# Sixteen modulation tiles and three short dependent chains: TensorE's early vector tiles placed around the second product, the last block finished one token half at a time

## The chip, the cores and the metric

The kernel runs on one core of one Trainium2 chip. The metric is the device time of one execution in microseconds (us); less is better. A core has five engines that run side by side, each through its own instructions in a fixed order: TensorE (PE, matrix products), VectorE (DVE), ScalarE (ACT), GpSimd (POOL) and SyncE (SP), whose queue starts most of the transfers from memory. An engine that meets an instruction whose input is not there waits, and everything behind it on that engine waits too.

## The reference

A decoder trunk with two layers, for 256 tokens of width 2048, in f32. Layer 0 mixes tokens with a causal conformer convolution, layer 1 with Mamba-2; each mixer is followed by a squared-ReLU MLP of inner width 8192. Cut to what matters:

```python
# layer i:
shift1, scale1, gate1, shift2, scale2, gate2 = split(silu(c) @ w_mod[i] + b_mod[i], 6)
u = rmsnorm(x, norm_mix_g[i]) * (1 + scale1) + shift1
x = x + gate1 * mixer(u)          # i = 0: conformer_conv, i = 1: mamba2
u = rmsnorm(x, norm_mlp_g[i]) * (1 + scale2) + shift2
x = x + gate2 * ((relu(u @ w1[i]) ** 2) @ w2[i])
# after both layers: rmsnorm(x, final_norm_g)

def conformer_conv(u, ...):
    v = u @ w_pw1 + b_pw1         # 2048 -> 4096
    a, gt = split(v, 2)
    v = causal_dwconv(a * sigmoid(gt), w_dw, b_dw)    # 31 taps
    return silu(layernorm(v, ln_g, ln_b)) @ w_pw2 + b_pw2

def mamba2(u, ...):               # at its end, for 8 groups of 512 channels:
    y = (y_scan + d_skip * xs) * silu(z)
    y = y * rsqrt(mean(y * y over the group) + eps) * norm_g
    return y @ w_out
```

The shifts, scales and gates are products of one vector, silu(c), with `w_mod` of 2048 x 12288 for each layer: much weight traffic for very little arithmetic. All weights come from memory once, as f32; for the products each is split into a rounded part `wh` and a remainder `wl`.

## The kernel before

The five products (pw1 and pw2 of the conformer, w1 and w2 of each MLP, w_in and w_out of Mamba) stream their weights in tiles of 1 MB (128 x 2048 f32) through SP's queue. ScalarE makes `wh` of a half tile (line 361), VectorE makes `wl` (line 363), and TensorE multiplies both with the activations. Activations stand transposed, channels on the partitions and tokens along the row; `block` and `outer` issue those products (line 376). Only the second product of the last MLP is made by `block_t` the other way round (lines 430 to 432): its result has 128 tokens on the partitions, `q` = 0 and 1 being the two token halves, and 512 columns for each of the four blocks `b`. One weight tile of that block has two halves, so a block has eight halves, and each half gives six matmuls for each token half: two weight rows `k` by three (`wh` with the rounded activations, `wl` with them, `wh` with their remainder).

The vector products for shift, scale and gate are spread over the program. A job is a triple (layer, segment, tile), and `gemv` carries it out: it starts the 1 MB load (`stream`, line 347) into a buffer with the tag `wm` (two buffers) or `hid` (four), and then either VectorE multiplies and sums it (line 292), or, for the groups in `PE_GROUPS`, TensorE does it with four matmuls (line 283). Four such tiles make a group: ScalarE copies their row of sums (line 289), and `columns` turns it into columns with four transposes (line 304) and a sum. `PE_GROUPS` holds the four groups of `SH2`, the shift of layer 0's MLP: 16 tiles. `EARLY` is the list of the jobs of layer 0's beginning in the order in which they are taken; `pump(n)` takes the next n of it. `RATE_PW1` (how many before each weight tile of pw1), then `BETWEEN` (within the LayerNorm between the convolution and pw2) and `RATE_PW2` (before each weight tile of pw2) say how many are taken where.

A list scheduler (`tc`) sets each engine's order from the order in the program, priorities and a cost model; `issue_after(x)` puts what is in it behind x, and loads keep program order on SP's queue.

Three places in the program are chains of small steps, each of which waits for the one before on another engine, while TensorE has little or nothing else to do:

- The LayerNorm ahead of pw2: sums over channels by matmuls with ones (line 801), mean and root (lines 819 to 824), then Silu (line 842) and the rounding of the first activations (line 485), with which TensorE starts pw2 (line 376).
- The RMSNorm between pw2 and the MLP's first product: squares of the new residual (line 536), sums over channels by matmuls with ones (`ms<-ones,sq`, line 512), root and reciprocal, a diagonal matrix (line 499) that is multiplied with ones (line 503) to give the factor on all partitions, and the first activations (lines 488 and 489). The same chain stands after the first MLP and after Mamba.
- The end: `into_rows` adds the last block to the residual (lines 1045 and 1049), squares it (line 1050) and multiplies it by the final norm's weight (line 1051); then the factor for all 256 tokens is made (lines 1349 to 1351), both token halves are multiplied by it (lines 1356 and 1358), and four transfers of 512 KB write the output (line 1359).

In Mamba, w_in is made in 20 blocks. After each half weight tile's products `step` takes one step of a list of generators, `self.todo`: `scores`, `scan` and, for each group, `gated`. `gated` multiplies y by silu(z) (lines 1297 and 1299), squares it (line 1306 in the DVE rows) and adds the squares up in halves (lines 1309 and 1310), lets two steps pass (`yield from lag(2)`), and then has TensorE sum over channels (line 512) within the stream of w_in's products.

Of the kernel before, what the change touches and what calls it, by code (L numbers as in the profile page):

```python
# [15 lines left out]
P = 128  # L16
# [28 lines left out]


RATE_PW1 = [1, 1, 1, 1, 1, 2, 1, 1, 1, 2, 1, 1, 1, 1, 0, 0]
BETWEEN = 5
RATE_PW2 = [1] * 12 + [2, 1, 2, 1]
RATE_OPEN = [1] * 9 + [0] * 3  # L50
RATE_MLP = spread(80, 116) + [0] * 50
RATE_OUT = spread(24, 32)
# [12 lines left out]

EARLY = [(0, s, 4 * g + i) for s, g in ((G1, 0), (G1, 1), (G1, 2), (SC2, 0), (SH2, 0), (SH2, 1)) for i in range(4)]
_te = [(0, SH2, 5 + i) for i in range(11)]
_ve = [(0, G1, 12 + i) for i in range(4)] + [(0, SC2, 4 + i) for i in range(12)]  # L70
_mix = _ve[:1]
for _i in range(5):
    _mix += [_te[2 * _i], _ve[1 + _i], _te[2 * _i + 1]]
EARLY = EARLY[:-3] + _mix + _te[10:] + _ve[6:]


PE_GROUPS = {(0, SH2, g) for g in range(4)}
# [96 lines left out]
def lag(n):  # L174

    for _ in range(n):
        yield


class Trunk:  # L180
# [226 lines left out]
                    if j % 2:  # L407
                        self.step()

    def block_t(self, src, rhs, evac, pump=None):  # L410


        banks = [self.bank(self.mm, "mm") for _ in range(2)]
        mm = self.nc.tensor.matmul
        for g in range(4):
            w = self.load_w(src[g])
            if pump:
                with nullcontext() if g else self.tc.issue_after(self.evac):
                    self.pump(pump(g))
            with self.tc.high_priority(self.ahead):  # L420
                parts = self.split_w(w)
            for i, (wh, wl) in enumerate(parts):
                last = g == 3 and i == 1
                order = [(q, k) for q in range(2) for k in range(2)] if last else [
                    (q, k) for k in range(2) for q in range(2)]
                for q, k in order:
                    t = 2 * i + k
                    hi = rhs[g][:, t, q * Q:(q + 1) * Q]
                    lo = rhs[g][:, t, T + q * Q:T + (q + 1) * Q]
                    mm(banks[q], lhsT=hi, rhs=wh[:, k, :], start=g == 0 and t == 0, stop=False)  # L430
                    mm(banks[q], lhsT=hi, rhs=wl[:, k, :], start=False, stop=False)  # L431
                    mm(banks[q], lhsT=lo, rhs=wh[:, k, :], start=False, stop=g == 3 and t == 3)  # L432
                    if last and k:
                        evac(q, banks[q])
                self.step()
                self.step()

    def step(self):

# [111 lines left out]
    def conformer(self):  # L551
# [310 lines left out]
        def make(g):  # L862
            if g:
                normed(g)
            if g == 3:
# [3 lines left out]
                for b in range(4):  # L869
# [8 lines left out]
        self.outer([a["pw2"][b] for b in range(3)], make, lambda b, j, parts: into[b](j, parts), pump,  # L878
                   there=[(there[0], [half]), (there[1], ()), (there[2], ())])
        self.block(a["pw2"][3], v, into[3], pump=pump, single=True)  # L880
        return res["ss"]


# [66 lines left out]
    def mlp(self, layer, ss, pump=None, after=None, first=None):  # L950
        nc, a = self.nc, self.a
        with self.tc.high_priority(AHEAD_CHAIN):
            r = self.rstd_bcast(ss, D)
        u = []
        st = {"acc": [None] * 4, "ss": []}
        gate = lambda b: self.mod_tile(layer, G2, b)
        self.sq_row = self.t("mom", [P, 2, 4], bufs=1)

        def make(g):
            self.need(layer, SC2, SH2, kg=g)  # L960
            with self.tc.high_priority(0 if g else AHEAD_CHAIN):
                u.append(self.modulate(r, layer, SC2, SH2, g))
            return u[g]

        for c in range(4):
            hid = [None] * 4

            def act(b, j, parts):
                if hid[b] is None:
                    self.rings = ("wm",)  # L970
                    hid[b] = self.b("hid", [P, 4, 2 * T], F32R)
                s = self.total(parts)
                q = self.t("a", [P, T], bufs=3)
                if len(parts) == 1:
                    nc.scalar.activation(out=q, in_=s, func=AF.Relu)
                    s = q
                    nc.vector.tensor_mul(q, q, q)
                else:
                    nc.vector.scalar_tensor_tensor(out=q, in0=s, scalar=0.0, in1=s, op0=ALU.max, op1=ALU.mult)
                self.split_x(hid[b], j, q)  # L980

            if c == 0:
                self.outer([a["w1"][layer, b] for b in range(OPEN)], make, act, first or (lambda g: 0))
                if layer == 1:
                    self.todo.append(self.to_rows())
            for b in range(0 if c else OPEN, 4):
                self.block(a["w1"][layer, 4 * c + b], u, lambda j, parts, b=b: act(b, j, parts), pump=pump)
            if layer == 1:
                for b in range(4):
                    self.block_t(a["w2"][layer, c, b], hid, self.into_rows(b, c == 3))  # L990
                continue
            for b in range(4):
                if c == 3:
                    self.need(layer, G2)
                if b < 3:
                    ev = self.into_h(st, b, gate, after, acc=False) if c == 3 else None
                    self.block_t(a["w2"][layer, c, b], hid, self.into_turned(st, b, c, ev), pump=pump)
                    continue
                ev = self.into_h(st, b, gate, after) if c == 3 else self.into_acc(st, b, c == 0)
                self.block(a["w2"][layer, c, b], hid, ev, pump=pump, single=c == 3)  # L1000
        assert not self.todo
        return st["ss"]
# [35 lines left out]
    def into_rows(self, b, last):  # L1038

        nc = self.nc  # L1040

        def evac(q, bank):
            h = self.ht[q][:, b * 512:(b + 1) * 512]
            v = self.t("t2", [P, 512], bufs=3)
            nc.vector.tensor_mul(v, bank, self.gate_row[b])
            if not last:
                nc.gpsimd.tensor_tensor(out=h, in0=h, in1=v, op=ALU.add)
                return
            nc.vector.tensor_add(h, h, v)
            nc.scalar.activation(out=v, in_=h, func=AF.Square, accum_out=self.sq_row[:, q, b:b + 1])  # L1050
            nc.vector.tensor_mul(h, h, self.fg_row[b])
        return evac


    def mamba(self, ss):
# [246 lines left out]
    def gated(self, g, c):  # L1302

        nc = self.nc
        y, z = c["x"], c["z"]
        nc.vector.tensor_mul(y, y, z)
        sq = z
        nc.scalar.activation(out=sq, in_=y, func=AF.Square)
        nc.vector.tensor_add(sq[:, :2, :], sq[:, :2, :], sq[:, 2:, :])
        nc.vector.tensor_add(sq[:, 0, :], sq[:, 0, :], sq[:, 1, :])  # L1310
        yield from lag(2)
        r = self.rstd_cols([sq[:, 0, :]], 512)
        yield
        rs = self.spread(r)
        if g < 4:
            dst = y
        else:
            dst = self.late[g] = self.b("acc", [P, 4, T], bufs=5)
        for j in range(4):
            nc.vector.scalar_tensor_tensor(out=dst[:, j, :], in0=y[:, j, :], scalar=self.col("norm_g", 4 * g + j),  # L1320
                                           in1=rs, op0=ALU.mult, op1=ALU.mult)
            if g < 4:
                self.split_x(self.out_hl[g], j, dst[:, j, :])
            if j == 1:
                yield from lag(3)
# [11 lines left out]
    def run(self, out):  # L1337
        nc = self.nc
        ss = self.conformer()
        self.spare = 0  # L1340
        self.queue_mod(0, G2)
        self.queue_mod(1, SC1, SH1, *LATER)
        rate, first = iter(RATE_MLP), iter(RATE_OPEN)
        ss = self.mlp(0, ss, pump=lambda g: next(rate), first=lambda g: next(first))
        ss = self.mamba(ss)
        last = iter(RATE_LAST)
        self.mlp(1, ss, pump=lambda g: 1, first=lambda g: next(last))
        r = self.t("rcol", [P, 2])
        nc.vector.reduce_sum(out=r, in_=self.sq_row, axis=mybir.AxisListType.X)
        nc.scalar.activation(out=r, in_=r, func=AF.Sqrt, scale=1.0 / D, bias=self.eps)  # L1350
        nc.vector.reciprocal(r, r)
        for i in range(2):
            for q in range(2):
                v = self.ht[q][:, i * 1024:(i + 1) * 1024]
                if q:
                    nc.scalar.mul(out=v, in_=v, mul=r[:, q:q + 1])
                else:
                    nc.vector.tensor_scalar_mul(out=v, in0=v, scalar1=r[:, q:q + 1])
                nc.sync.dma_start(out=out[q, :, i * 1024:(i + 1) * 1024], in_=v)


def build(nc, tc, a, out):
    with ExitStack() as ctx:
# [17 lines left out]
```

## Time and profile before

| what | us |
| --- | --- |
| median of 3 runs | 2592.21 |
| the runs | 2587.94 to 2595.47 |
| profiled execution, its own time | 2593.28 |
| span of the profiled execution | 2591.2 |
| TensorE busy | 2540.7 |
| VectorE busy | 1910.9 |
| ScalarE busy | 1311.4 |

A row of the timeline reads: start and duration in us, engine, line, operation, output `<-` inputs, sizes, number of instructions, and in brackets how long the engine was idle before it and what released it. Matmuls are pipelined, so that the start of the next one, not the duration, gives the pace. A row of the table by stretches gives its length, then for each engine the busy time and the number of instructions, the clock that TensorE was granted (1.00 is full speed), the mean busy share of the 16 transfer engines, and what they moved in GB/s. The name before `<-` in a transfer is the buffer, the one behind it the array in memory. An instruction of SP in the timeline is the issue of a transfer; its landing is told apart.

### The profile page before, as it was taken

The page shows a single profiled execution, that of the slowest core. Times are in us where ns is not written, and L with a number is a line of the kernel's source. Part 1 is how long each engine was busy: PE and PEld are TensorE (multiplying, and loading weights), DVE is VectorE, ACT ScalarE, POOL GpSimd, SP SyncE. Part 2 cuts the span into 40 slices and gives each one's busy share as a digit, 9 for nine tenths or more (in the row PEclk, how much of TensorE's full clock was granted, in tenths as well). Part 3 has the DMA queues.
Part 4 walks back from the last instruction along what each step waited for, and adds up shares of the span by engine and source line. Part 5 has one row for each costly group of instructions (what it writes and reads, how often), then busy time and mean ns, then how long its engine had stood idle before and what let it go on. Part 6 is the DMA issues. An engine that isn't in the chain of part 4 may idle for free.

```text
span 2591.2 us, 36890 instructions
## 1 busy us (share of the span) xinstructions
PE 2540.7 (98%) x14671; PEld 2184.0 (84%) x14671; DVE 1910.9 (74%) x2460; ACT 1311.4 (51%) x2011; POOL 147.0 (6%) x212
## 2 busy tenths in 40 slices
PE   7999999999999999999999999999999999999998
PEld 5887698988888888888888888888998888888886
DVE  6579577877878878888777777898885555565565
ACT  2067453544434434447777667744454444443443
POOL 0011000000000000000000000000001101101000
PEclk8999999999999999999999999999999999999999
DMA  9988797788888878856555455688765555555553
GB/s 404 381 322 305 266 344 300 284 326 311 313 329 316 324 287 346 320 216 221 172 194 175 167 189 194 233 310 326 294 245 192 195 181 193 194 182 194 193 184 141
DMA packets 94895, 664.85 MB, mean 257 GB/s; under 512 B 10977, under 2 KB 10977, under 8 KB 16769
## 3 DMA queue, kind: packets, MB, share of 16 engines
q1 hardware_dynamic: 89138, 643.87, 67.4%
q0 software_dynamic: 5152, 16.97, 2.4%
q8 instruction: 115, 1.88, 0.3%
q10 hardware_dynamic: 432, 1.66, 0.2%
q14 instruction: 58, 0.48, 0.0%
HBM read 657.02 MB, written 2.20 MB: 254 GB/s over the span
## 4 chain that ended last, share of the span: by engine, by line
PE 93%; DVE 3%; DMA 2%; ACT 1%; issue 1%; POOL 0%; ACTq 0%; SPq 0%; DVEq 0%
PE mm L376 58%; PE mm L430 8%; PE mm L431 8%; PE mm L432 8%; PE mm L712 7%; DMA hid<-wmT 1%; PE mm L658 1%; DVE wl L363 1%; PE ms L712 1%; DMA wm<-wmT 1%; PE ms L1293 0%; PE ms L283 0%; DMA t<-eac_d 0%; DVE hid L292 0%; ACT wh L361 0%
## 5 line engine op out<-in xcount | busy, mean ns | idle before, releaser
L376 PE MATMUL mm<-u,wh 128*128 128x512 f32 (+1 forms) x4544 | 1376.5, 365 | 4.4 <-ACT u L485 2.3
L363 DVE TENSOR_TENSOR wl<-w,wh 128x1024 fp32r<-128x1024 f32 x768 | 942.2, 1229 | 506.1 <-ACT wh L361 500.3
L361 ACT CAST wh<-w 128x1024 fp32r<-128x1024 f32 x768 | 806.1, 1050 | 975.2 <-PE mm L376 589.5
L376 PE MATMUL mm<-u,wl 128*128 128x256 f32 x3840 | 1081.0, 282 | 0.1
L376 PEld LDWEIGHTS mm<-u,wh 128*128 128x128 f32 x4544 | 812.6, 190 | 156.1 <-issue 6.6
L376 PEld LDWEIGHTS mm<-u,wl 128*128 128x128 f32 x3840 | 730.5, 190 | 5.8 <-issue 2.5
L430 PE MATMUL mm<-wh,hid 128*128 128x512 f32 x896 | 351.0, 392 | 0.0
L432 PE MATMUL mm<-wh,hid 128*128 128x512 f32 x896 | 348.9, 389 | 0.0
L431 PE MATMUL mm<-wl,hid 128*128 128x512 f32 x896 | 348.8, 389 | 0.0
L292 DVE SCALAR_TENSOR_TENSOR wm<-wm,scb 128x2048 f32<-128x2048 f32 x132 | 301.7, 2286 | 11.4 <-DMA wm<-wmT 11.2
L712 PE MATMUL mm<-u,w 128*128 128x256 f32 x864 | 191.8, 383 | 18.7 <-ACT u L586 18.7
L712 PEld LDWEIGHTS mm<-u,w 128*128 128x128 f32 x864 | 164.7, 192 | 45.1 <-ACT u L586 19.9
L430 PEld LDWEIGHTS mm<-wh,hid 128*128 128x128 f32 x896 | 168.3, 188 | 35.8 <-issue 1.0
L431 PEld LDWEIGHTS mm<-wl,hid 128*128 128x128 f32 x896 | 168.3, 188 | 35.3 <-issue 0.7
L432 PEld LDWEIGHTS mm<-wh,hid 128*128 128x128 f32 x896 | 168.3, 188 | 35.1
L376 PE MATMUL mm<-hid,wh 128*128 128x512 f32 (+1 forms) x576 | 182.3, 373 | 0.0
L376 PE MATMUL mm<-hid,wl 128*128 128x256 f32 x512 | 144.1, 281 | 0.0
L292 DVE SCALAR_TENSOR_TENSOR hid<-hid,scb 128x2048 f32<-128x2048 f32 x44 | 100.5, 2287 | 41.7 <-DMA hid<-wmT 41.5
L376 PEld LDWEIGHTS mm<-hid,wh 128*128 128x128 f32 x576 | 104.1, 189 | 20.3 <-ACT u L485 0.2
L320 POOL TENSOR_TENSOR mod<-mod,par 128x4 f32<-128x4 f32 x46 | 37.1, 806 | 1128.8 <-DVE wm L292 915.2
L605 ACT ACTIVATE taps<-u,par 128x256 f32<-128x256 f32 x224 | 93.1, 500 | 9.2 <-DVE taps L614 6.7
L376 PEld LDWEIGHTS mm<-hid,wl 128*128 128x128 f32 x512 | 97.0, 190 | 0.4 <-issue 0.2
(251 smaller groups left out, 1606.0 us busy)
## 6 DMA issues: line engine op xcount, KB each, us to landing
w<-w SPq DMA_DIRECT2D x256, 1024.0 KB, 4.9
wm<-wmT SPq DMA_DIRECT2D x139, 1024.0 KB, 7.3
w<-win SPq DMA_DIRECT2D x80, 1024.0 KB, 4.9
hid<-wmT SPq DMA_DIRECT2D x53, 1024.0 KB, 10.5
w<-pw SPq DMA_DIRECT2D x46, 1024.0 KB, 6.9
w<-wout SPq DMA_DIRECT2D x32, 1024.0 KB, 6.9
acc<-ac_d POOLq DMA_DIRECT2D x16, 512.0 KB, 8.0
xpad<-u POOLq DMA_DIRECT2D x24, 131.5 KB, 8.1
```

The source lines that it names most:

```text
L292: self.sum = nc.vector.scalar_tensor_tensor(out=w, in0=w, scalar=1.0, in1=self.scb, op0=ALU.mult, op1=ALU.mult, accum_out=m[:, i:i + 1]).ins
L320: nc.gpsimd.tensor_tensor(out=m, in0=m, in1=b, op=ALU.add)
L361: nc.scalar.copy(out=wh, in_=w[:, s, :])
L363: nc.vector.tensor_tensor(out=wl, in0=w[:, s, :], in1=wh.bitcast(F32), op=ALU.subtract)
L376: self.pe = self.nc.tensor.matmul(out, lhsT=lhsT, rhs=rhs, skip_group_check=True, **kw).ins
L430: mm(banks[q], lhsT=hi, rhs=wh[:, k, :], start=g == 0 and t == 0, stop=False)
L431: mm(banks[q], lhsT=hi, rhs=wl[:, k, :], start=False, stop=False)
L432: mm(banks[q], lhsT=lo, rhs=wh[:, k, :], start=False, stop=g == 3 and t == 3)
L605: st["tap"] = nc.scalar.activation(out=p4[:, q, :], in_=vp[:, k + q:k + q + T], func=AF.Identity, scale=self.col("w_dw", ct * TAPS + k + q ...
L658: self.pe = nc.tensor.matmul(o[32 * c:32 * c + 32, :], lhsT=w[:, k, 32 * c:32 * c + 32], rhs=r[:, c, k:k + T], start=k == 0, stop=k == 7, ...
L712: self.pe = nc.tensor.matmul(o, lhsT=w[:, t, j * P:(j + 1) * P], rhs=u[g][:, t, :], start=g == 0 and t == 0 and j < 2, stop=g == 3 and t == 3,
```

## The change

Three edits:

- `EARLY` has a new order, and other numbers are taken at each place. In the LayerNorm seven `SH2` tiles are taken instead of five, in pw2 twelve jobs instead of 18 (five `SH2` tiles instead of eleven, and seven VectorE tiles as before), and a new `BEHIND` takes the last four `SH2` tiles behind pw2's last block, which is the RMSNorm ahead of the MLP.
- The last block of the last product takes `tail=5`: halves 5, 6 and 7 are kept back, and their 36 matmuls are issued with the 18 of token half 0 first. `into_rows` then ends each token half by itself (`rows_out`), with its own factor and its two output transfers. VectorE takes a half's first 1024 and last 512 columns, ScalarE the 512 between.
- `gated` lets three steps pass instead of two between its squares and their sum.

```diff
-BETWEEN = 5
-RATE_PW2 = [1] * 12 + [2, 1, 2, 1]
+BETWEEN, BEHIND = 7, 4
+RATE_PW2 = [1, 1, 1, 0] * 4
...
-EARLY = [(0, s, 4 * g + i) for s, g in ((G1, 0), (G1, 1), (G1, 2), (SC2, 0), (SH2, 0), (SH2, 1)) for i in range(4)]
-_te = [(0, SH2, 5 + i) for i in range(11)]
+_te = [(0, SH2, i) for i in range(16)]
 _ve = [(0, G1, 12 + i) for i in range(4)] + [(0, SC2, 4 + i) for i in range(12)]
-_mix = _ve[:1]
+EARLY = [(0, G1, i) for i in range(12)] + [(0, SC2, i) for i in range(4)] + _te[:7]
 for _i in range(5):
-    _mix += [_te[2 * _i], _ve[1 + _i], _te[2 * _i + 1]]
-EARLY = EARLY[:-3] + _mix + _te[10:] + _ve[6:]
+    EARLY += [_ve[_i], _te[7 + _i]]
+EARLY += _ve[5:7] + _te[12:] + _ve[7:]
...
-    def block_t(self, src, rhs, evac, pump=None):
+    def block_t(self, src, rhs, evac, pump=None, tail=8):
...
+            for i, hl in enumerate(parts, 2 * g):
+                if i >= tail:
+                    late.append((i, hl))
+                    continue
...
+        if late:
+            for q in range(2):
+                for i, hl in late:
+                    for k in range(2):
+                        sums(q, i, k, *hl)
...
         self.block(a["pw2"][3], v, into[3], pump=pump, single=True)
+        with self.tc.issue_after(self.pe):
+            self.pump(BEHIND)
...
-                    self.block_t(a["w2"][layer, c, b], hid, self.into_rows(b, c == 3))
+                    self.block_t(a["w2"][layer, c, b], hid, self.into_rows(b, c == 3), tail=5 if c == b == 3 else 8)
...
+    def rows_out(self, q, f):
+        nc = self.nc
+        r = self.t("rcol", [P, 2])[:, :1]
+        nc.vector.reduce_sum(out=r, in_=self.sq_row[:, q, :], axis=mybir.AxisListType.X)
+        nc.scalar.activation(out=r, in_=r, func=AF.Sqrt, scale=1.0 / D, bias=self.eps)
+        nc.vector.reciprocal(r, r)
+        row = self.ht[q]
+        nc.vector.tensor_scalar_mul(out=row[:, :1024], in0=row[:, :1024], scalar1=r)
+        nc.scalar.mul(out=row[:, 1024:1536], in_=row[:, 1024:1536], mul=r)
+        nc.vector.tensor_scalar_mul(out=row[:, 1536:], in0=f, scalar1=r)
+        for i in range(2):
+            cs = slice(i * 1024, (i + 1) * 1024)
+            nc.sync.dma_start(out=self.out[q, :, cs], in_=row[:, cs])
...
-        yield from lag(2)
+        yield from lag(3)
```

What this makes of the engines' orders is shown at three places. In these rows the numbers behind the names count buffers and differ between the two kernels, and the line numbers of the changed kernel are a few off: its line 282 is line 283 before, 375 is 376, 523 is 512, 514 is 503.

On SP's queue around the LayerNorm, before (`wm` and `hid` from `wmT` are vector tiles, `w` from `pw` is a weight tile of pw2; the first two rows are the fourth and fifth of the tiles that TensorE takes in the LayerNorm):

```order
L347 DMA wm_1928<-wmT 128x2048
L347 DMA hid_1936<-wmT 128x2048
L347 DMA w_267_1944<-pw 128x2048
L347 DMA wm_1952<-wmT 128x2048
L347 DMA hid_2008<-wmT 128x2048
```

And after:

```order
L346 DMA wm_1928<-wmT 128x2048
L346 DMA hid_1936<-wmT 128x2048
L346 DMA wm_1944<-wmT 128x2048
L346 DMA hid_1950<-wmT 128x2048
L346 DMA w_269_1956<-pw 128x2048
L346 DMA hid_1964<-wmT 128x2048
```

The loads of the sixth and seventh tile now stand ahead of pw2's weight tile. The sixth goes into a `wm` buffer, of which there are two; the buffer is that of the second tile.

On TensorE at the same place, before, from the third tile into pw2:

```order
L283 MATMUL ms_1911<-hid_1922,scol 32x512 x4
L283 MATMUL ms_1911<-wm_1928,scol 32x512 x4
L283 MATMUL ms_1939<-hid_1936,scol 32x512 x4
L376 MATMUL mm_1946<-u_1887,wh_1904 128x256
L376 MATMUL mm_1947<-u_1887,wh_1904 128x256
```

And after:

```order
L282 MATMUL ms_1911<-wm_1928,scol 32x512 x4
L282 MATMUL ms_1939<-hid_1936,scol 32x512 x4
L282 MATMUL ms_1939<-wm_1944,scol 32x512 x4
L375 MATMUL mm_1958<-u_1887,wh_1904 128x256
L375 MATMUL mm_1959<-u_1887,wh_1904 128x256
```

The sixth tile's four matmuls stand ahead of pw2's first, the seventh's thirteen rows behind it.

On TensorE in the RMSNorm ahead of the MLP, before (`ones` with `ssum` or `sq` are the sums of squares, `diag` is the factor's matrix, and the last row is the MLP's first product):

```order
L512 MATMUL ms_3123<-ones,ssum_2648 128x1 x2
L512 MATMUL ms_3123<-ones,sq_3103 128x1 x2
L376 MATMUL mm_2836<-u_2554,wh_3057 128x256 x2
L376 MATMUL mm_2836<-u_2554,wl_3058 128x256
L512 MATMUL ms_3123<-ones,sq_3112 128x1 x2
L512 MATMUL ms_3123<-ones,sq_3121 128x1 x2
L503 MATMUL ms_3137<-diag_3135,ones 128x256
L376 MATMUL mm_3140<-u_3146,wh_3171 128x256
```

And after:

```order
L282 MATMUL ms_3098<-hid_3095,scol 32x512
L523 MATMUL ms_3123<-ones,ssum_2648 128x1 x2
L523 MATMUL ms_3123<-ones,sq_3075 128x1 x2
L523 MATMUL ms_3123<-ones,sq_3084 128x1 x2
L282 MATMUL ms_3098<-hid_3095,scol 32x512 x3
L282 MATMUL ms_3098<-wm_3103,scol 32x512
L523 MATMUL ms_3123<-ones,sq_3093 128x1 x2
L282 MATMUL ms_3098<-wm_3103,scol 32x512 x3
L282 MATMUL ms_3098<-hid_3109,scol 32x512 x4
L282 MATMUL ms_3098<-hid_3115,scol 32x512 x4
L514 MATMUL ms_3137<-diag_3135,ones 128x256
L375 MATMUL mm_3140<-u_3146,wh_3171 128x256
```

Sixteen matmuls of the last four tiles stand between the sums, eleven of them behind the last sum and ahead of the product with `diag`.

On VectorE in `gated` of the first group, before (line 1240 is a mask added in another generator, 363 are splits of w_in's weights, 1306 to 1310 the squares and their halves):

```order
L1297 SCALAR_TENSOR_TENSOR wm_9823<-wm_9823,par,ms_10390 128x256 x2
L1240 TENSOR_TENSOR acc_10549<-acc_10549,mask 128x1024
L1299 TENSOR_TENSOR wm_9823<-wm_9823,t_1544_10245 128x4x128
L363 TENSOR_TENSOR wl_10461<-w_1578_10454,wh_10460 128x1024
L1306 TENSOR_TENSOR wm_9823<-wm_9823 128x1024
L363 TENSOR_TENSOR wl_10522<-w_1587_10519,wh_10521 128x1024
L1309 TENSOR_TENSOR wm_9823<-wm_9823 128x512
L1310 TENSOR_TENSOR wm_9823<-wm_9823 128x256
```

And after (1330 to 1343 are lines 1297 to 1310 of before):

```order
L1330 SCALAR_TENSOR_TENSOR wm_9823<-wm_9823,par,ms_10390 128x256 x2
L1332 TENSOR_TENSOR wm_9823<-wm_9823,t_1544_10245 128x4x128
L1339 TENSOR_TENSOR wm_9823<-wm_9823 128x1024
L362 TENSOR_TENSOR wl_10455<-w_1576_10448,wh_10454 128x1024
L1342 TENSOR_TENSOR wm_9823<-wm_9823 128x512
L1343 TENSOR_TENSOR wm_9823<-wm_9823 128x256
```

The mask and one split no longer stand between the gating and the squares. On TensorE the sum over channels of this group stands 13 matmuls nearer to the products of the generators ahead of it than before, since the scheduler has moved those as well.

More of the change, by code (lines that the diff above doesn't have):

```diff
@@ L408, in block, with sums @@
                         self.step()
-    def block_t(self, src, rhs, evac, pump=None):
+    def block_t(self, src, rhs, evac, pump=None, tail=8):
         banks = [self.bank(self.mm, "mm") for _ in range(2)]
         mm = self.nc.tensor.matmul
+        late = []
+        def sums(q, i, k, wh, wl):
+            g, t = i // 2, 2 * (i % 2) + k
+            hi = rhs[g][:, t, q * Q:(q + 1) * Q]
+            lo = rhs[g][:, t, T + q * Q:T + (q + 1) * Q]
+            mm(banks[q], lhsT=hi, rhs=wh[:, k, :], start=i == 0 and k == 0, stop=False)
+            mm(banks[q], lhsT=hi, rhs=wl[:, k, :], start=False, stop=False)
+            mm(banks[q], lhsT=lo, rhs=wh[:, k, :], start=False, stop=i == 7 and k == 1)
+            if i == 7 and k:
+                evac(q, banks[q])
         for g in range(4):
@@ L421, in block_t @@
                 parts = self.split_w(w)
[L422 to L434, printed above, removed]
+            for i, hl in enumerate(parts, 2 * g):
+                if i >= tail:
+                    late.append((i, hl))
+                    continue
+                for q, k in [(q, k) for q in range(2) for k in range(2)] if i == 7 else [
+                        (q, k) for k in range(2) for q in range(2)]:
+                    sums(q, i, k, *hl)
                 self.step()
                 self.step()
+        if late:
+            for q in range(2):
+                for i, hl in late:
+                    for k in range(2):
+                        sums(q, i, k, *hl)
     def step(self):
@@ L1050, in evac @@
             nc.scalar.activation(out=v, in_=h, func=AF.Square, accum_out=self.sq_row[:, q, b:b + 1])
-            nc.vector.tensor_mul(h, h, self.fg_row[b])
-        return evac
+            if b < 3:
+                nc.vector.tensor_mul(h, h, self.fg_row[b])
+                return
+            f = self.t("t2", [P, 512], bufs=3)
+            nc.vector.tensor_mul(f, h, self.fg_row[b])
+            self.rows_out(q, f)
+        return evac
+    def rows_out(self, q, f):
[11 more added lines that the diff above has]
+            nc.sync.dma_start(out=self.out[q, :, cs], in_=row[:, cs])
     def mamba(self, ss):
@@ L1346, in run @@
         last = iter(RATE_LAST)
+        self.out = out
         self.mlp(1, ss, pump=lambda g: 1, first=lambda g: next(last))
[L1348 to L1359, printed above, removed]
 def build(nc, tc, a, out):
```

## The prediction

> **What bounds the kernel now.** I read the page first: busy shares, the clock in forty slices, the chain that ended last.
>
> ```profile
> span 2591.2 us, 36890 instructions
> ...
> PE 2540.7 (98%) x14671; PEld 2184.0 (84%) x14671; DVE 1910.9 (74%) x2460; ACT 1311.4 (51%) x2011; POOL 147.0 (6%) x212
> ...
> PEclk8999999999999999999999999999999999999999
> ...
> PE 93%; DVE 3%; DMA 2%; ACT 1%; issue 1%; POOL 0%; ACTq 0%; SPq 0%; DVEq 0%
> ```
>
> TensorE is busy for 2540.7 of 2591.2 us. So an edit can win time in three ways only: fewer matmuls on that stream, less of the 50 us in which it stands still, or less time at a lowered clock, which the page's tenths are too coarse to show. I therefore went on to TensorE's timeline, and read every idle gap with its releaser, then stretches around the gaps for the clock.
>
> ```profile
> 304.37 1.06 PE L283 MATMUL ms<-hid,scol 128*32 128x512 f32 x8
> ...
> 307.83 1.04 PE L283 MATMUL ms<-hid,scol 128*32 128x512 f32 x8
> 311.15 0.85 PE L376 MATMUL mm<-u,wh 128*128 128x256 f32 x3 [2.28 <-ACT u L485]
> ...
> 420.84 0.61 PE L512 MATMUL ms<-ones,sq 128*128 128x1 f32 x4 [0.69 <-ACT sq L536]
> 422.69 1.19 PE L503 MATMUL ms<-diag,ones 128*128 128x256 f32 x2 [1.24 <-DVE diag L499]
> 424.99 1.22 PE L376 MATMUL mm<-u,wh 128*128 128x256 f32 x4 [1.11 <-ACT u L488]
> ...
> 1252.76 0.99 PE L512 MATMUL ms<-ones,wm 128*128 128x1 f32 x4 [2.54 <-DVE wm L1310]
> ...
> 1382.80 0.58 PE L512 MATMUL ms<-ones,wm 128*128 128x1 f32 x4 [0.70 <-DVE wm L1310]
> ```
>
> These are the gaps that the change touches: 2.28 us in the LayerNorm, 3.04 in the RMSNorm behind pw2, 2.54 and 0.70 at the channel sums of two gated groups. The clock around them:
>
> ```profile
> 306.46:309.87 3.41, 2.41 (x24) 0.52 (x16) 2.71 (x5) 1.95 (x3) 0.00 (x0) 1.00 0.73 231
> 309.87:313.28 3.41, 2.13 (x16) 1.97 (x17) 2.12 (x7) 3.41 (x9) 0.00 (x0) 1.00 0.94 351
> 419.10:422.51 3.41, 1.66 (x14) 1.49 (x13) 1.05 (x4) 2.14 (x4) 0.00 (x0) 1.00 0.21 87
> 422.52:429.32 6.80, 5.36 (x20) 4.38 (x21) 6.38 (x12) 2.11 (x5) 0.00 (x0) 0.50 0.66 253
> 1248.54:1251.95 3.41, 1.63 (x8) 0.90 (x6) 3.41 (x4) 2.92 (x7) 0.00 (x0) 1.00 0.61 196
> 1251.96:1258.76 6.80, 6.00 (x21) 5.35 (x22) 2.50 (x6) 5.57 (x8) 0.00 (x0) 0.50 0.70 249
> ```
>
> The columns are the stretch, its length, the busy time of PE, weight loads, DVE, ACT and POOL, the granted clock, and transfers. Two stretches of 6.8 us stand at half clock, and each follows a stretch of 3.41 us in which TensorE was busy for 1.66 or 1.63 us. Their starts, 422.51 and 1251.95, are 829.44 us apart, which is 243 times 3.413. I read this as a fixed grid of 3.41 us: a square of it that is half idle is paid with the next two at half speed. The LayerNorm's gap lies across a line of that grid (309.87 is 33 steps ahead of 422.51), which leaves 1.00 us idle in one square and 1.28 in the next, and the clock held at 1.00. So it counts how much of a gap falls into one square, and a longer gap in the same place is another matter.
>
> [...]
>
> **The tiles in pw2.** Eleven TensorE tiles stand within pw2's stream before and six after (the seventh of the LayerNorm and five). The price of one:
>
> ```profile
> 331.39 0.40 PE L376 MATMUL mm<-u,wh 128*128 128x256 f32 x2
> 331.63 0.28 PE L376 MATMUL mm<-u,wl 128*128 128x256 f32 x1
> 331.84 1.06 PE L283 MATMUL ms<-wm,scol 128*32 128x512 f32 x8
> 332.83 0.50 PE L376 MATMUL mm<-u,wh 128*128 128x256 f32 x2
> 333.17 0.28 PE L376 MATMUL mm<-u,wl 128*128 128x256 f32 x1
> ```
>
> Two matmuls of the stream take 0.24 us (331.39 to 331.63). From 331.63 to 333.17 are 1.54 us with three of them (0.36), so that a tile costs 1.18 us where the stream is full. Five fewer: −5.9 us. TensorE has no gap in pw2 before, so all of it shortens the path if nothing else becomes late. VectorE's tiles in pw2 stay seven, and the same megabytes come through SP's queue, in another order. I keep −5.3 to −6.5.
>
> **The sixth tile in the LayerNorm.** Five tiles run at 0.86 us each (304.37 to 307.83 is four) and end at about 308.7, when the second has long given back its `wm` buffer. The slot for the next `wm` load is there in the trace:
>
> ```profile
> 306.36 0.33 SPq L347 DMA_DIRECT2D wm<-wmT  x1
> 306.79 1.99 SPq L347 DMA_DIRECT2D hid<-wmT  x2
> ...
> L347 SPq DMA_DIRECT2D wm<-wmT x1: 328/328/328, 306.4 to 306.4; - x1
> ...
> DMA to landing us min/median/max: 6.4/6.4/6.4
> ...
> L347 SPq DMA_DIRECT2D wm<-wmT x1: 328/328/328, 1701.6 to 1701.6; - x1
> ...
> DMA to landing us min/median/max: 4.7/4.7/4.7
> ```
>
> Before, this load was for pw2. After, it carries the sixth tile, which stands ahead of pw2's first matmul. Issued at 306.36 with two more behind it, it landed 6.4 us later, at 312.76; a load of the same kind that had the queue to itself took 4.7 us, which would be 311.06. Then come 0.86 us of tile, and pw2 starts at 313.6 (or 311.9) instead of 311.15. I take +2.5 us, since the queue stands as in the first row; the lower end is +0.8. Behind the waiting tile on TensorE is all of pw2; the seventh tile lands about as far behind as one megabyte takes, 3 us at the 351 GB/s of the stretch from 309.87, while thirteen rows run. pw2's third weight tile goes behind both loads and is needed only with the third block's products; I cost it at nothing.
>
> With a landing at 312.76 the square from 309.87 to 313.28 is idle for 2.9 of 3.41 us, more than the 1.75 and 1.78 that were enough elsewhere. So the next two squares, 6.8 us of pw2, go at half speed: 3.4 us if TensorE is full all the time, 3.0 by the row of 1251.96 (6.00 busy). I take +3.0; with the early landing 1.2 us of that square are idle and it is 0. This term has the most doubt.
>
> **Four tiles in the RMSNorm behind pw2.** They go where TensorE waits anyway (0.69, 1.24 and 1.11 us), so their own time is mostly covered. But eleven of their matmuls stand between the last sum and the product with the diagonal: at 0.215 us each 2.4 us behind the sum at 420.84, which with its 0.43 gives 423.7 instead of 422.69, +1.0. What is late next is the first w1 product. In return the square up to 422.51 is full, and the half clock from 422.52 goes: the diagonal product takes 0.6 rather than 1.19, and the 4.3 us from 424.99 to 429.32 could take half. VectorE was busy for 6.38 of those 6.80 us, so I count 1.5 for both. −0.5 us, between −1.2 (all of the clock is won) and +0.5 (nothing but the wait).
>
> **Gated groups.** For the first group VectorE's and TensorE's orders move against each other.
>
> ```profile
> 1246.25 1.22 DVE L1240 TENSOR_TENSOR acc<-acc,mask 128x1024 f32<-128x1024 f32 x1
> ...
> 1249.12 1.22 DVE L1306 TENSOR_TENSOR wm<-wm 128x1024 f32<-128x1024 f32 x1
> ...
> 1252.19 0.42 DVE L1310 TENSOR_TENSOR wm<-wm 128x256 f32<-128x256 f32 x1
> ```
>
> A mask (1.1 us to the next start) and one split, also about 1.1, no longer stand ahead of the squares, so the last halving ends about 2.1 us earlier than at 1252.6. But TensorE reaches the sum 13 matmuls earlier, at 0.22 us some 2.8 us. So the wait of 2.54 becomes about 3.2, and the clock still drops: +0.7 us. Ends: −0.8 and +2.2, a split or two more or less ahead. For the other groups I count nothing.
>
> **The end.**
>
> ```profile
> 2578.15 0.39 PE L432 MATMUL mm<-wh,hid 128*128 128x512 f32 x1
> ...
> 2578.58 0.69 DVE L1045 TENSOR_TENSOR t<-mm,h 128x512 f32<-128x512 f32 x1
> ...
> 2580.03 0.63 ACT L1050 ACTIVATE t<-wm 128x512 f32<-128x512 f32 x1 [0.64 <-DVE wm L1049]
> ...
> 2582.11 1.42 DVE L1358 TENSOR_SCALAR wm<-wm,rcol 128x1024 f32<-128x1024 f32 x2
> ...
> L1359 SPq DMA_DIRECT2D out<-wm x4: 343/604/1176, 2582.9 to 2584.6; - x4
> ...
> DMA to landing us min/median/max: 2.7/4.9/5.6
> ```
>
> The last matmul stays at 2578.15, because the number of matmuls is the same. The four outputs are issued from 2582.9 to 2584.6, and the last lands at 2590.2. After, token half 0 ends some 4 us earlier (18 matmuls), and its two transfers are away before half 1's. Half 1 still goes through add, square, root and multiplication: its square starts at 2580.03 and is summed by 2580.8, reduction, root and reciprocal take about 0.7, so the multiplications start near 2581.5 instead of 2582.11. The first 1024 columns take 0.71 (half of 1.42); issues near 2582.3 and 2582.75. With two half megabytes instead of four in flight the last lands between 2586.2 (3.4 us behind its issue) and 2587.7 (4.9, the median of the four). I take 2586.9: −3.3 us, between −2.5 and −4.0.
>
> **The sum.** −5.9 + 2.5 + 3.0 − 0.5 + 0.7 − 3.3 = −3.5 us, against the profiled execution's 2593.28: 2589.8. That execution lay 1.07 us above the median of the three runs, 2592.21, so I predict 2588.7. If every term is at its good end, with the early landing and no drop, it is −6.5 + 0.8 + 0 − 1.2 − 0.8 − 4.0 = −11.7; at its bad end −5.3 + 2.5 + 3.4 + 0.5 + 2.2 − 2.5 = +0.8.
>
> **Rivals.**
> - The sixth tile is no wait to speak of: it lands near 311.1, the clock holds. For it: 4.7 us has been seen; against it: the row of 6.4 has the same neighbours in the queue. The two terms become 0.8 and 0, −8.2 in all: 2584.0. Chance 0.22.
> - The gated wait shrinks below what drops the clock. It needs VectorE 0.8 us earlier than I count, for instance by one more split moved behind the squares. Then the 2.54 is at most about 1.7 and the half clock goes: −0.8 − 3.0 instead of +0.7: 2584.2. Chance 0.12; together with the first, 2579.5, 0.04 more.
> - Slower: the sum of the squares comes too early in other groups as well. The row at 1382.80 shows a sum that waited 0.70 us. If TensorE gets to this one and to another some 2 us sooner, as to the first, each has a wait of about 2.7 and pays 3.0 of half clock: 5.0 and 5.7, together +10.7: 2599.4, and 2602 with the bad ends of two other terms. It decides from a wait of 1.75 us within one square on. Against it: VectorE's squares come earlier in all groups. Chance 0.07.
> - The end does not do what it says: half 1's transfers queue behind half 0's and land as late as before. Then −0.2 in all: 2592.0. Against it: half 0's would be issued near 2578.3, 4 us ahead. Chance 0.07.
>
> That leaves 0.48 for the forecast. A measurement of this kernel tells about 0.3%, 7.8 us, from no change, which puts the bounds at 2584.4 and 2600.0. Faster: two thirds of the first two rivals (0.22), their joint case (0.04) and a little of the forecast (0.02), 0.28. Slower: the third rival's upper half and the drift of three runs, 0.07. Same: 0.65. For 8 in 10 the range takes in both faster rivals and most of the third: 2579 to 2597.
>
> **What would show it.** In the trace after: TensorE's gap ahead of the sixth tile, 3 to 4 us from 308.7 on, and half clock from 313.3 to 320; pw2 from its first to its last product 5.9 us shorter but for that; no half clock behind pw2 and w1's products about half a microsecond late; the gated sum's gap near 3.2 us with half clock behind it; two pairs of output issues, four microseconds apart, and the last landing 8.7 us behind the last matmul's start instead of 12.1. I am wrong if the clock holds in pw2, or if pw2 has a gap of its own, with VectorE or a weight load as releaser.

## The result: 6 to 7 us slower

| | median, us | runs | range |
| --- | --- | --- | --- |
| before | 2592.29 | 22 | 2587.94 to 2598.44 |
| changed | 2599.17 | 22 | 2592.54 to 2602.35 |

The ratio is 1.0024, with an interval of 1.0017 to 1.0031: +6 us by the ratio (+4.4 to +8.0), +6.9 by the medians. I had predicted 2588.7. The lines of the changed kernel's page that answer to those shown of before:

```profile
span 2597.6 us, 36899 instructions
...
PE 2545.6 (98%) x14671; PEld 2181.9 (84%) x14671; DVE 1911.9 (74%) x2464; ACT 1310.6 (50%) x2013; POOL 145.7 (6%) x212
...
PEclk8999999999999999999999999999999999999999
```

The shares differ by one point at most; the clock in tenths and the count of matmuls are those of before. TensorE is busy 4.9 us longer, and the span is 6.4 us longer. To see where, I set the two traces against each other on TensorE: both have the same 5264 matmuls with a `wl` half, in nearly the same order, and the k-th of the one less the k-th of the other says how far the changed kernel is behind at that point. This table is worked out from the two traces, at places in the program:

| place (time before, us) | changed less before, us | step |
| --- | --- | --- |
| first products of pw2 (312) | +4.8 | +4.8 |
| pw2 at 353 | +5.1 | +0.4 |
| end of pw2 (414) | −0.5 | −5.6 |
| first MLP, 434 | +1.0 | +1.5 |
| first MLP, 514 | +3.1 | +2.1 |
| end of the first MLP (1142) | +4.0 | +0.9 |
| near the end of w_in (1643) | −1.6 | −5.6 |
| end of w_out (1849) | +11.1 | +12.7 |
| second MLP to the last product (2578) | +10.4 | −0.7 |
| end of the span (2591.2) | +6.4 | −4.0 |

One row is much larger than anything that I had in the sum: w_out, whose own code the change leaves as it is, loses 12.7 us. The other rows first, each with the lines that answer to those of the prediction.

In the LayerNorm (TensorE's timeline, the sixth tile's load, and stretches, all of the changed kernel):

```profile
308.08 1.04 PE L282 MATMUL ms<-hid,scol 128*32 128x512 f32 x8
313.92 1.94 PE L282 MATMUL ms<-wm,scol 128*32 128x512 f32 x8 [4.80 <-DMA wm<-wmT]
315.79 1.01 PE L375 MATMUL mm<-u,wh 128*128 128x256 f32 x3
...
L346 SPq DMA_DIRECT2D wm<-wmT x1: 328/328/328, 306.6 to 306.6; - x1
...
DMA to landing us min/median/max: 7.3/7.3/7.3
...
309.55:312.95 3.40, 0.00 (x0) 0.00 (x0) 2.14 (x6) 2.99 (x8) 0.00 (x0) 1.00 0.99 352
312.97:319.77 6.80, 5.85 (x28) 3.90 (x32) 4.17 (x5) 2.65 (x4) 0.00 (x0) 0.50 1.01 422
```

The sixth tile's load was issued at 306.61, as foreseen, landed 7.3 us later, and TensorE stood for 4.80 us; the square of 3.4 us ahead of 312.95 is wholly idle and the next 6.8 us run at half clock.

In the RMSNorm behind pw2:

```profile
421.59 0.61 PE L523 MATMUL ms<-ones,sq 128*128 128x1 f32 x4
422.12 1.06 PE L282 MATMUL ms<-wm,scol 128*32 128x512 f32 x3
422.95 1.08 PE L282 MATMUL ms<-wm,scol 128*32 128x512 f32 x3
423.00 3.60 PE L282 MATMUL ms<-hid,scol 128*32 128x512 f32 x15
426.52 0.70 PE L514 MATMUL ms<-diag,ones 128*128 128x256 f32 x2
428.34 0.91 PE L375 MATMUL mm<-u,wh 128*128 128x256 f32 x3 [1.11 <-ACT u L499]
```

The idle time is gone (but for 1.11 us), since the tiles fill it; but they stand ahead of the diagonal product, which starts 4.93 us behind the last sum's start instead of 1.85 before, and w1 begins at 428.34 instead of 424.99.

At the gated sums of groups 0 and 6:

```profile
1254.66 0.65 PE L523 MATMUL ms<-ones,wm 128*128 128x1 f32 x4 [3.29 <-DVE wm L1343]
...
1661.45 0.58 PE L523 MATMUL ms<-ones,wm 128*128 128x1 f32 x4 [1.13 <-DVE wm L1343]
...
1255.05:1258.46 3.41, 3.41 (x12) 2.93 (x12) 1.25 (x4) 1.28 (x3) 0.00 (x0) 0.50 0.66 271
1258.46:1261.87 3.41, 3.41 (x23) 3.08 (x22) 2.83 (x6) 1.32 (x3) 0.00 (x0) 1.00 0.32 46
```

Group 0 waits 3.29 us, about the 3.2 of the prediction. But the half clock behind it lasts one square of 3.41 us, not two as before, and so this place wins: from 1240 to 1259 the changed kernel goes from 3.8 us behind to 2.6. And the end:

```profile
2584.90 0.69 DVE L1058 TENSOR_TENSOR t<-mm,h 128x512 f32<-128x512 f32 x1 [1.77 <-PE mm L423]
...
2588.98 0.69 DVE L1058 TENSOR_TENSOR t<-mm,h 128x512 f32<-128x512 f32 x1
...
L1085 SPq DMA_DIRECT2D out<-wm x4: 332/356/383, 2588.6 to 2593.1; - x4
...
DMA to landing us min/median/max: 2.6/3.1/3.5
```

Token half 0's last steps start 4.08 us ahead of half 1's, the landings take 3.5 us at most instead of 5.6, and the span ends 9.1 us behind the last matmul's start (2588.55) instead of 13.1.

### The profile page after: what moved, and what is told of

The parts are those of the page before. It is cut to its first block, busy times and chain, and to the rows that moved or that the text cites. A ratio compares the mean times of both kernels' runs of the same rounds, so it can differ in the third digit from the quotient of the medians.

```text
span 2597.6 us, 36899 instructions
## 1 busy us (share of the span) xinstructions
PE 2545.6 (98%) x14671; PEld 2181.9 (84%) x14671; DVE 1911.9 (74%) x2464; ACT 1310.6 (50%) x2013; POOL 145.7 (6%) x212
## 4 chain that ended last, share of the span: by engine, by line
PE 91%; DVE 4%; DMA 3%; ACT 1%; issue 1%; POOL 0%; SPq 0%; DVEq 0%; ACTq 0%
PE mm L375 55%; PE mm L421 8%; PE mm L423 8%; PE mm L422 8%; PE mm L723 7%; DVE wl L362 1%; DMA hid<-wmT 1%; PE mm L669 1%; PE ms L723 1%; DVE hid L291 1%; PE ms L282 1%; DMA w<-wout 1%; DMA wm<-wmT 1%; PE ms L1326 0%; ACT wh L360 0%
```

## What w_out shows

w_out over 100 us, before and then changed (the columns are length, PE, weight loads, DVE, ACT, POOL, clock, share of the transfer engines, GB/s):

```profile
1660.00:1760.00 100.00, 100.00 (x599) 87.17 (x597) 93.19 (x122) 57.66 (x87) 2.93 (x5) 1.00 0.82 310
```

```profile
1660.00:1760.00 100.00, 94.66 (x551) 78.85 (x550) 88.50 (x124) 54.55 (x86) 2.75 (x4) 1.00 0.70 274
```

Before, TensorE never stops in these 100 us, and VectorE is busy for 93% of them: it splits w_out's weights, adds up results and takes vector jobs of layer 1, of which all of w_out has 24 at 2.29 us. In the changed kernel both are busy for less, and TensorE issues 551 matmuls instead of 599. From 1643 to 1849 the 12.7 us divide so, by the two traces: TensorE is idle for 5.7 us instead of 0.0; the groups' own matmuls there are 87 instead of 67, and take 2.4 us more, which w_in is spared; and w_out's products follow each other more slowly, 4.6 us in all. What stands differently there are the last two groups. The halving of group 6's squares on VectorE, before:

```profile
1640.26 0.42 DVE L1310 TENSOR_TENSOR wm<-wm 128x256 f32<-128x256 f32 x1
```

and changed:

```profile
1660.88 0.42 DVE L1343 TENSOR_TENSOR wm<-wm 128x256 f32<-128x256 f32 x1
```

It is 20.6 us later, while TensorE's stream is 1.6 us ahead there. Counting `yield`s in the code explains a part of it. Every `step` takes the next piece of the first generator in the list, whichever group it belongs to. A block takes 16 steps (two for each half weight tile, not one), so w_in's 20 blocks have 40 steps for each of the 8 groups, and a step lasts 25.5 / 16 = 1.6 us. A group's generators take 17 (`scores`) + 18 (`scan`) + 6 (`gated`) = 41 before (group 0 takes 44), and 42 with one more in `gated`. Once group 0 has begun, the list never runs empty, so the extra steps add up: group 6's squares stand six steps later than before (9.6 us) and its sum seven, group 7's seven and eight. Counted so, group 6 ends at step 312 of w_in's 320 instead of 305, and group 7 runs 34 steps into w_out instead of 26. The diff says "one step more"; the program makes it eight at the end. On VectorE the delay does not grow evenly: the last halvings of groups 0 to 7 start 1.9, 12.8, 4.7, 5.0, 9.7, 0.5, 20.6 and 18.2 us later than before. The scheduler's order and the waits come on top of the steps; how much each gives was not tried.

Two waits follow. The first is on SP's queue between 1600 and 1760 (total, times, longest): in the changed kernel the vector tile that stands ahead of w_out's third weight tile waits 13.5 us for a `wm` buffer that group 6 still holds, where it did not wait before (the 8.9 us of before are at group 7). Before and changed:

```profile
SPq L347 <- DVE acc L1320: 8.9, 1, 8.9
```

```profile
SPq L346 <- DVE acc L1353: 17.4, 2, 13.5
```

The second is on VectorE, which multiplies a scan's result with factors that come by a transfer (line 1284, now 1317), and stands still until they land; between 1628 and 1760, before and then changed:

```profile
DVE t L1284 <- DMA t<-eac_d: 2.9, 1, 2.9
```

```profile
DVE t L1317 <- DMA t<-eac_d: 10.9, 2, 6.2
```

VectorE stands still for 8 us more here; in the 100 us above it had 6.8 us to spare.

## The experiments

Two theories stood at first: that the extra step in `gated` makes w_out late (step theory), and that the moved early tiles do, through the vector jobs behind them (tile theory). Ratios are against runs of the kernel before in the same batch.

**The extra step taken back, and alone.**

```diff
 # x1: the changed kernel
-        yield from lag(3)
+        yield from lag(2)
 # x2: the kernel before
-        yield from lag(2)
+        yield from lag(3)
```

> The changed kernel with the gated groups' wait put back to two steps. Step theory: a group's generators take 41 steps before and 42 in the changed kernel, while w_in offers 40 for each group, so every group ends a step (1.6 us) later than the one before it, the last two run into w_out, and w_out loses about 11 us while w_in gains about 5. Then undoing it gives about 7 us: 2592 us, 0.0 to +0.05% against the kernel before, with the RMSNorm behind pw2 still 3.6 us slower and the end 4 us faster. Tile theory: the loss in w_out comes from the other places of the early tiles, through later vector jobs; then this stays near 2599.

> The kernel before with three steps instead of two in gated, nothing else. Step theory: +7 us, 2599, and w_out's products start as late as in the changed kernel (about 12 us lost there, 5 won in w_in). Tile theory: within 1 us of before.

Measured: x1 2589.38 us, ratio 0.9989 (0.9980 to 0.9998); x2 2602.27 us, ratio 1.0037 (1.0024 to 1.0049). One number in the code costs 9 to 10 us, whichever way it is tried, somewhat more than the 7 that I read from the two profiles. In x2's trace w_in ends 5.3 us ahead of before and w_out 9.5 behind; within w_out it has 3.4 us at half clock, from 1721.8 (its granted clock is 0.98 from 1660 to 1760), which the changed kernel's trace has not (1.00 in the row above). The tile theory has fallen.

**The end alone, the early tiles alone.** x3 is the kernel before with `tail=5` and `rows_out`; x4 is the kernel before with the new `EARLY`, `BETWEEN`, `RATE_PW2` and `BEHIND`.

> The kernel before with only the end changed (the last block one token half at a time, with its own output transfers). By the profile of the changed kernel, whose last landing came 9.3 us behind the last matmul's start instead of 13.1: -4 us, 2588. If what the end won there was only that the transfers met less traffic at that moment: 0 to -2.

> The kernel before with only the early tiles moved. By sums over the changed kernel's trace: LayerNorm +5.1, pw2 -5.6, RMSNorm and the first products behind it +3.6, mlp +1.0: +4 us, 2596. Tile theory: it also has w_out's loss, +11 to +15.

Measured: x3 2588.24 us, 0.9982 (0.9974 to 0.9991): −4.7 us (−6.7 to −2.3), as the profile's −4.0. x4 2592.63 us, 1.0004 (0.9994 to 1.0014): +1 us, less than the +4 that I read from one trace, and no difference that these runs can tell. The three parts add up: −4.7 + 1.0 + 9.6 = +5.9, against the +6 measured for all three.

**Is it the number of steps, or the pause in each `gated`?**

```diff
 # x5: the kernel before, in gated
-        yield from lag(2)
+        yield from lag(2 if g else 10)
 # x6: the kernel before, in gated and at the end of scan
-        yield from lag(2)
+        yield from lag(3)
...
-        yield from lag(2)
+        yield from lag(1)
```

> The kernel before, with ten steps instead of two between squares and sum in group 0 alone, and two in all the others. Step theory (what counts is how many steps all groups together have taken by the end): groups 6 and 7 come as late as in the changed kernel, w_out loses about 11 us, and w_in wins about as much as with three steps everywhere: +8 to +11, 2600 to 2603. If it is the place of the later groups' own sums that costs: those are as before, group 0's wait of 2.54 us and its half clock go, and the time falls by 3 to 5: 2588.

> The kernel before with three steps in gated and one step instead of two at the end of scan, just ahead of it, so that a group takes 41 steps as before. Step theory: the loss is gone; the time is that of before within 2 us, since sum and squares stand as before and only the gating is taken up a step earlier. If a longer pause within gated itself costs (the buffer that it holds for one step more): +8 to +10, as with three steps alone.

Measured: x6 2592.48 us, 1.0000 (0.9992 to 1.0009). The pause in `gated` is three steps as in x2, the sum of steps is 41, and the loss is gone: it is the sum that counts. x5 2594.77 us, 1.0005 (0.9996 to 1.0014), so both expectations missed. Its trace shows why. It wins 5.5 us at group 0 (from 1240 to 1280), where neither the wait of 2.54 us nor the half clock is left, and then w_out loses as it does with three steps everywhere: by 1639 it is 5.6 us ahead of before, by 1800 5.7 behind. The step theory had the loss right and group 0's gain too small.

**SP's queue, or VectorE's time?** Within w_out two causes were left: weights that stand in SP's queue behind a vector tile whose buffer is not free, or VectorE, that has no room. x7 keeps vector tiles out of the first quarter of w_out; x9 moves eight of them to the first MLP.

```diff
 # x7: the changed kernel
-RATE_OUT = spread(24, 32)
+RATE_OUT = [0] * 8 + spread(24, 24)
 # x9: the changed kernel
-RATE_MLP = spread(80, 116) + [0] * 50
-RATE_OUT = spread(24, 32)
+RATE_MLP = spread(88, 116) + [0] * 50
+RATE_OUT = spread(16, 32)
```

> The changed kernel, but with no vector job ahead of the first eight weight tiles of w_out, and one ahead of each of the other 24. SP theory: w_out starves since its weight loads stand in SP's queue behind a vector tile whose buffer group 6 still holds; then most of the loss goes, 2591 to 2594. Rival: VectorE and ScalarE have the last two groups' steps to do while they split w_out's weights, and the queue only follows; then 2597 to 2601.

> The changed kernel with 8 of the 24 vector jobs of w_out done in the first MLP instead (88 there, 16 in w_out). VectorE theory: w_out loses because VectorE, busy for 147 of 160 us there before, has no room for what the last two groups bring with them; 8 jobs of 2.3 us less make 18 us of room, and at least 6 us of the loss in w_out go: 2592 or less, if the first MLP takes the 8 at no cost. Rival: the last groups' chains block TensorE, ScalarE and the queues whatever VectorE has to do; then 2597 to 2600.

Measured: x7 2600.41 us, 1.0027 (1.0017 to 1.0037): nothing won. In its trace the first quarter does run better (from 1639 to 1720 it loses 3.0 us, the changed kernel 8.1), but the jobs are only put off, and the stretch behind loses instead: TensorE is busy for 95.09 of its 100 us, VectorE for 91.58:

```profile
1760.00:1860.00 100.00, 95.09 (x584) 83.25 (x582) 91.58 (x110) 38.43 (x48) 0.79 (x4) 1.00 0.87 349
```

x9 2589.73 us, 0.9996 (0.9987 to 1.0005): 0.28% (7.3 us) faster than the changed kernel. The same 100 us of w_out as above:

```profile
1660.00:1760.00 100.00, 98.16 (x584) 84.33 (x584) 84.38 (x116) 55.19 (x86) 3.47 (x4) 1.00 0.72 272
```

And VectorE's waits at the scans in x9:

```profile
DVE t L1317 <- PE mm L375: 5.7, 1, 5.7
DVE t L1317 <- DMA t<-eac_d: 4.6, 1, 4.6
```

They are about as long as in the changed kernel, 10.3 us together, of which 4.6 are put down to the transfer. The long wait in SP's queue is there as well (in x9, 1600 to 1760):

```profile
SPq L346 <- DVE acc L1353: 13.9, 2, 13.5
```

Yet from 1639 to 1840 x9 loses 6.2 us, the changed kernel 12.2. So neither wait alone sets the loss: with eight vector jobs fewer in w_out about half of it goes. That speaks for VectorE's time, but does not part it from the queue, since each job also brings 1 MB through SP's queue. In w_out (1639 to 1850) ScalarE's split waited for its weights, before, changed, x7 and, in x9, not at all:

```profile
ACT wh L361 <- DMA w<-wout: 2.8, 1, 2.8
```

```profile
ACT wh L360 <- DMA w<-wout: 14.7, 5, 7.4
```

```profile
ACT wh L360 <- DMA w<-wout: 31.1, 11, 4.3
```

Late weights are thus a part of the loss; whether they come late because a slow VectorE gives buffers back late, or because of the queue's order, was not tried with VectorE's work held the same. Nor was it tried how the remaining 6 us divide.

**Where the early tiles went.** x8 and x11 are the changed kernel with two steps in `gated` and other numbers of tiles in the LayerNorm, in pw2 and behind it: 5, 7, 4 in x8 and 7, 9, 0 in x11, where x1 has 7, 5, 4.

> The changed kernel with two steps in gated, and five early tiles in the LayerNorm instead of seven, seven in pw2 instead of five, four behind pw2 as in the changed kernel. If the sixth tile's wait is what the LayerNorm lost (4.3 us idle ahead of it in the run with two steps, and half clock behind it): 4.3 + 0.9 + up to 1.7 won, less about 0.7 that the gap has without it being filled and two tiles at 1.18 us: about 3 us faster than that run, 2586.5. If pw2 waits for the sixth tile at its new place as long as the LayerNorm did: the same as that run, 2589 to 2591.

> The changed kernel with two steps in gated, seven early tiles in the LayerNorm, nine in pw2 and none behind it. By the prediction the four tiles behind pw2 gained 4.7 in pw2 and 0.5 behind it, so without them the run is 5 us slower than that with two steps: 2594. By the changed kernel's trace (RMSNorm and first products +3.6, first MLP +1.0) they gained nothing: 2589 to 2590.

Measured: x8 2588.63 us, 0.9982 (0.9974 to 0.9991); x11 2588.19 us, 0.9985 (0.9974 to 0.9996); x1 was 0.9989 (0.9980 to 0.9998), and the kernel before with the end alone 0.9982. All four overlap. Four tiles behind pw2, two more in the LayerNorm, or none of it: no difference that these runs show. The 2594 that the prediction's prices gave for x11 is outside its runs. x8 lost its wait for the sixth tile but not the 2.28 us of the LayerNorm itself, and pays two tiles in pw2.

**A version that beats both.** x10 is the kernel before with the new end, ten steps in group 0 and one step less at the end of `scan` in groups 1 to 7; x12 adds five, nine and two early tiles.

```diff
 # x10 and x12, in gated and at the end of scan
-        yield from lag(2)
+        yield from lag(2 if g else 10)
...
-        yield from lag(2)
+        yield from lag(1 if g else 2)
```

> The kernel before with the changed end, ten steps instead of two between squares and sum in group 0 alone, and one step instead of two at the end of scan in groups 1 to 7, so that the last groups stand one step later than before instead of eight. Step theory: the end gives 4, and group 0's wait of 2.5 us and its half clock (up to 3 us) go without a loss in w_out: 2584 to 2586. If group 0's wait only moves to another group: 2588, as with the end alone.

> As the kernel with the end, group 0's ten steps and the shorter scan, and five early tiles in the LayerNorm, nine in pw2 and two behind it, which stand ahead of the sums and not behind them. 2 x 1.18 us less in pw2 and no delay of the diagonal product: 1 to 2.5 us faster than that kernel, 2582 to 2584. If the sums are what the two tiles push back: the same.

Measured: x10 2583.95 us, 0.9970 (0.9958 to 0.9981); x12 2583.76 us, 0.9966 (0.9954 to 0.9979). 8 to 9 us faster than before and 14 to 15 faster than the changed kernel; the two extra tiles behind pw2 add nothing that can be told. Where group 0 waited, x10 has no gap and full clock:

```profile
1248.00:1262.00 14.00, 14.00 (x83) 12.21 (x82) 11.26 (x17) 10.04 (x15) 0.00 (x0) 1.00 0.67 226
```

## Why the prediction was wrong

Its own steps, with the size given and what the traces or runs showed:

| step | predicted | shown |
| --- | --- | --- |
| five fewer tiles in pw2 | −5.9 | −5.6, from 353 to 414 |
| wait for the sixth tile, and the half clock behind it | +5.5 | +5.1 by 353 |
| four tiles behind pw2 | −0.5 | +3.6 by 514 |
| gated groups | +0.7 | w_in −5.6 (of it group 0 −1.2), w_out +12.7 by the traces; 9 to 10 in all by the runs |
| the end | −3.3 | −4.0 in the trace, −4.7 alone |

- **The step that failed is "For the other groups I count nothing".** I worked out group 0, where the trace had a gap. The wait came out right (3.2 us foreseen, 3.29 shown), its price did not: with one square of half clock instead of two the place won 1.2 us instead of losing 0.7. For the others I looked only at how squares and sum stand to each other, not at where the groups stand in the program. The count was there to be made: 41 steps in a supply of 40, so one step more for each of eight groups. That this ends in w_out, where VectorE is busy for 93% of the time (the row of before above), can be read in the profile of before; the size, 9 to 10 us, can't. The rival on the slower side named later groups too, but by another mechanism (sums that come too early, and their half clock). The changed kernel's trace doesn't show it: the one other wait at a group's sum that it has is group 6's 1.13 us, at full clock. That this rival's 2599.4 lies next to the measured 2599.17 is luck.
- **The four tiles behind pw2** were priced by the wrong end of the chain. I let eleven matmuls follow the last sum at once, at 0.215 us each. The last sum itself came later (421.59 instead of 420.84), the row of 15 at 423.00 takes 3.6 us, and another 1.1 us still wait behind the diagonal product. The half clock behind the idle time of before (6.8 us from 422.52) went mostly, as foreseen (one square, 422.2 to 425.6, was left), but w1's first products then waited for VectorE's activations at 465.15 and 482.60, 0.97 us together. I had named this end, +0.5, as the worst.
- **The LayerNorm** came out as forecast, with its parts shifted: the wait was longer, 4.80 us instead of 3.9. In other executions of the same edit it was 4.31 (x1), 3.73 (x4) and 2.34 (x9). The first rival's price for it rested on a misread row: the load of 4.7 us did not have the queue to itself, since a weight tile was issued 0.44 us behind it, at 1702.06. Nor do the loads behind it decide: with the same loads behind it the sixth tile took 7.3 us here and 4.8 in x9. What makes the difference stays open.
- **The end** was a little better than forecast: the landings took 3.5 us at most, where I had taken between 3.4 and 4.9. The 4.9 is the median of before; the 3.4 was an estimate that no row shows, and the four landings of before lie between 2.7 and 5.6.

The range, 2579 to 2597, ended 2 us below the median measured. With every term at its bad end the sum gives 2593.0, and the range went on to 2597 for the third rival; the term that I had priced at nothing was the largest.

## What to carry to other kernels

When work is fed into a stream by a list of small steps, add up the steps that it takes and the steps that the stream offers before moving one: in a list that never runs empty one more step per item adds up from item to item, and here it was paid where the list runs on into a stage in which VectorE had little to spare (6.8 of 100 us). Look for the cost of a delay in the stage after the one that is changed, by the busy share of every engine there, not of the bounding one alone. And work that is put into a chain's idle time delays the chain if it stands between one of its steps and the next: in the changed kernel's trace the diagonal product came 3.1 us later behind the last sum. The runs can't tell the cost of that from nothing.

## What the runs showed of the hardware

Between the first 44 us and the end of the last product, the stretches of half clock in the two traces start on a grid of 3.413 us (829.44 / 243). In before they start at 422.51, 1149.55, 1251.95 and 1856.11, which are 213, 30 and 177 steps apart; with the changed kernel at 312.95, 422.18, 1152.63, 1255.03 and 1866.02, which are 32, 214, 30 and 179 steps apart. They last one step of it (3.41 us, at 422.18 and 1255.03 of the changed kernel) or two (6.8 us, at all the others).

The grid did not lie at the same place of the program in two executions. I had read the LayerNorm's gap of 2.28 us as harmless because it lay across a line of the grid. In x2, whose program is the same up to there, the same gap was followed by half clock (timeline and stretch of x2):

```profile
312.01 1.04 PE L376 MATMUL mm<-u,wh 128*128 128x256 f32 x3 [2.28 <-ACT u L485]
...
312.13:315.53 3.40, 3.40 (x16) 3.37 (x17) 2.56 (x6) 3.40 (x7) 0.00 (x0) 0.50 1.01 419
```

So the same gap of 2.28 us was paid in one execution and not in the other: in x2 all of it (309.73 to 312.01) lies in one square (308.72 to 312.12), in before (308.87 to 311.15) a line at 309.87 divided it, and the clock was 1.00 from 306.46 to 313.28. The rule of the prediction, that a square half idle is paid, is not the whole of it. In before TensorE was idle for 2.0 us of one square, and the next ran at full clock:

```profile
94.80:98.20 3.40, 1.42 (x7) 1.22 (x8) 2.55 (x5) 1.82 (x4) 0.20 (x1) 1.00 1.02 422
98.27:101.68 3.41, 3.41 (x18) 3.00 (x17) 3.41 (x3) 0.00 (x0) 0.00 (x0) 1.00 1.02 423
```

And in the RMSNorm of the changed kernel half clock followed a square in which the trace shows no idle time:

```profile
418.78:422.18 3.40, 3.40 (x30) 2.15 (x32) 1.23 (x1) 1.35 (x2) 0.00 (x0) 1.00 0.29 118
422.18:425.59 3.41, 3.41 (x20) 0.84 (x22) 1.82 (x3) 1.20 (x2) 0.00 (x0) 0.50 0.88 291
```

What else counts stays open. That one gap of 2.28 us had two outcomes is a reason to read such a gap's clock cost as a chance and not as a sum. Where the grid lies can also be part of why 22 executions of one kernel differ by 10 us (2587.94 to 2598.44 before), which was not tried by itself.
